# Token sums of two pairs at once, one more pair-of-pairs by seven products, and a first product fed in pieces

## The chip, the cores and the metric

The kernel runs on one core of a Trainium2 chip. The core has TensorE (PE: matrix products; PEld is its loading of the stationary operand), VectorE (DVE), ScalarE (ACT), GpSimd (POOL) and SyncE (SP), which work at the same time and wait for each other by semaphores. Transfers are issued from the queues of SP, ScalarE and POOL and carried by 16 DMA engines. The metric is the time of one execution on the device in microseconds (us).

## What is computed

One layer of a decoder for 256 tokens of width 2048, in float32:

```
h    = rmsnorm(x, g_mix);  proj = h @ w_in          # 2048 x 15872
x_r, g_r, q, k, v, gate_r, gate_a = split(proj)
y_r  = (gelu(g_r) * rg_lru(conv(x_r))) @ w_rnn_out  # 2816 wide
y_a  = stick_breaking_attention(norm(q), norm(k), v) @ w_attn_out
x    = x + (sigmoid(gate_r) * y_r + sigmoid(gate_a) * y_a) @ w_o
g, u = split(rmsnorm(x, g_ffn) @ w_ffn_gu)          # 2 x 5632 wide
x    = x + (silu(g) * u) @ w_ffn_down
x    = x + sigmoid(rmsnorm(x, g_ple) @ w_ple_gate) * (p @ w_ple_proj)
```

All weights are read once from HBM; the products of 256 tokens with them are nearly all of the arithmetic.

## The kernel before

**Products in split form.** TensorE takes float32 rounded to a shorter format (fp32r). Every operand is therefore split into a rounded part and the rest: ScalarE copies it to fp32r (`whi`, `shi`), VectorE subtracts that from the original (`wlo`, `slo`). A product is three matmuls, hi x hi, hi x lo, lo x hi, added up in PSUM (`prod`, line 207). A plain product has a tile of 128 x 128 token values as the stationary operand and 512 weight columns as the moving one. A weight tile is 128 x 1024 values, 512 KB: one load, one ScalarE copy, one VectorE subtraction.

**Groups.** `group` (line 757) computes 256 tokens times 1024 columns over all rows of a weight matrix. The rows are taken in tiles of 128, and two tiles are a pair. A pair is done plainly, by eight products (2 row tiles x 2 column halves x 2 token halves), or, where the configuration `CFG` lists it, by seven products of sums (Strassen's scheme, names `11`, `21`, `22`, `T1` to `T4`). `CFG` lists 196 pairs. The seven-product form needs sums of weight blocks and sums of token blocks.

- The weight sums `T1` to `T4` are made on VectorE (`r<-r,r`, 1024 columns), or, where the `how` list names them, by a transfer of POOL that adds a block from HBM onto the one in SBUF (`add`, line 192). Two pairs share each of these tiles.
- The token sums are made by `half_sums` (line 714) for one pair at a time: one VectorE instruction on 256 columns, two on 128, a ScalarE copy of 512 and a VectorE subtraction of 512. For the input x the unsplit tile `h` is first put together again from its two parts by VectorE (`x_sums`, line 883).

**Order of the work.** `build` writes the whole layer down as a list of operations. TensorE's come in the order of the program: the projection groups (five for the recurrent branch, a half one, two for gate_r, the recurrent output between them), then v, q and k, gate_a, the attention output, `w_o`, eleven groups for the gate and up matrices with the down products between them, and the last gate. Hooks put transposes and attention steps between the products; the positions are `att0`, `every`, `at` and `turn`. `schedule` (line 308) then plays this list through with estimated durations and with the buffers that there are (`ROOM`: 54 tiles of 1024 columns, 8 PSUM banks): each of the other engines takes what is ready in the order of due times, which are counted back from the product that needs it. TensorE may take a product up to 60 places ahead. `improve` (line 508) repeats this up to 20 times with earlier due times for whatever made TensorE wait. The result is a fixed order per engine. Waits between engines follow from the data and from buffers used again.

**The start.** Nine products on zeros (`warm`, line 648) run first. ScalarE's queue loads the 16 columns of factors `gm`. SP's queue loads the first x tile in two halves and the weights of the first two row tiles as four pieces of 512 columns. ScalarE and VectorE scale and split x (`gained`, line 705).

**The end.** The last of the four output pieces is computed in two halves of 256 columns and stored by SP (`store`, line 188), one store behind the other.

```
717:        q = tile("hs", "H")
720:        pr.vec(2 * P, lambda nc: nc.vector.tensor_tensor(
721:            R3(2)(q[:2 * P].ap()), R3(2)(h[:2 * P].ap()), R3(3)(h[P:].ap())[:, ::2, :], ALU.subtract),
723:        tt(s2, s1, a11, ALU.subtract, name="hs")
724:        tt(s4, a12, s2, ALU.add, name="hs")
725:        t = split(q.all, name)
```

Of the kernel before, what the change touches and what calls it, by code (L numbers as in the profile page):

```python
# [91 lines left out]
class Program:  # L92
# [95 lines left out]
    def store(self, dst, i, kb, name="", writes=(), cap=None):  # L188
        return self.op("SP", 0.06, 0.0, lambda nc: nc.sync.dma_start(dst(nc), i.ap()), [i], list(writes), size=kb,
                       name=name, cap=cap)  # L190
# [397 lines left out]
def order_of(ks, nd, lead=0):  # L588
# [24 lines left out]
def build(cfg):  # L613
# [11 lines left out]

    gm = const("gm", KD)
# [22 lines left out]
    pr.mms([(warm[i % 8].all, ones_r.all, nil.all, 0.4, True, True) for i in range(9)], [ones_r.all, nil.all],  # L649
# [21 lines left out]
    def load_x(i, halves=False):  # L671
        xt[i] = tile("xt", "H")
        for e in range(2) if halves else (None,):
            o = xt[i].all if e is None else xt[i][e * 256:e * 256 + 256]
            pr.load(o, dram("xT", (lambda e: lambda a: a[:, 2 * i:2 * i + 2, :].rearrange("p k s -> p (k s)")
                                   if e is None else a[:, 2 * i + e, :])(e)), 256 if e is None else 128, name="xt")

    load_x(0, True)
# [26 lines left out]
    def gained(src, gain, name):  # L705
        t = tile(name, "L", dt=F32R)
        for e in range(2):
            s = slice(e * 256, e * 256 + 256)
            g = gain[e:e + 1]
            act(t[s], src[s], AF.Identity, scale=g, name=name)  # L710
            stt(t[512 + e * 256:768 + e * 256], src[s], g, t[s].f32(), ALU.mult, ALU.subtract, name=name)
        return t

    def half_sums(h, name):


        q = tile("hs", "H")
        a11, a12 = h[:P], h[2 * P:3 * P]
        s3, s1, s2, s4 = (q[c * P:c * P + P] for c in range(4))
        pr.vec(2 * P, lambda nc: nc.vector.tensor_tensor(  # L720
            R3(2)(q[:2 * P].ap()), R3(2)(h[:2 * P].ap()), R3(3)(h[P:].ap())[:, ::2, :], ALU.subtract),
               [h.all], [q[:2 * P]], name="hs")
        tt(s2, s1, a11, ALU.subtract, name="hs")
        tt(s4, a12, s2, ALU.add, name="hs")
        t = split(q.all, name)
        return [(t[c * P:c * P + P], t[512 + c * P:640 + c * P]) for c in (1, 2, 0, 3)]
# [30 lines left out]
    def group(w, cols, ks, pairs, sums, tokens, how, hooks=None, lead=0):  # L757
# [7 lines left out]
        early = {x for x in order if x[0] in "AB"} if lead and nd else ()  # L765
# [13 lines left out]
        for n, x in enumerate(order):  # L779
# [3 lines left out]
            m, dp = x[:2]  # L783
            if m in ("A", "B"):
# [95 lines left out]
    for i in range(NPD):  # L880
        xg.append(gained(xt[i].all, gm[2 * i:2 * i + 2], "xg"))

    def x_sums(ps):
        for p in ps:
            if p not in xsum:
                h = tile("h", "H")
                tt(h.all, xg[p][:512].f32(), xg[p][512:].f32(), ALU.add, name="h")
                xsum[p] = half_sums(h, "xs")

    x_sums(xp)  # L890
    for b in range(4):
        for t in range(2):
            q = tile("xq", "H")
            pr.load(q.all, dram("x", (lambda t, b: lambda a: a[t * P:t * P + P, b * 512:b * 512 + 512])(t, b)), 256,
                    name="xq", early=None)
# [35 lines left out]
    xc, xcs, y, ysum, hr = {}, {}, [], {}, {}  # L931

# [54 lines left out]
    def finish(p):  # L987
# [4 lines left out]
        tt(r.all, ps.all, r.all, ALU.mult, name="y")  # L992
        y.append(split(r.all, "y"))
        if p in union("ro"):
            ysum[p] = half_sums(r, "ys")
# [114 lines left out]
    heads, osum = {}, {}  # L1110
    qs, ks_, zst, ost = {}, {}, {}, []
# [95 lines left out]
    def att_o(hp):  # L1207
# [18 lines left out]
        if hp in union("ao"):  # L1226
            h = tile("h", "H")
            act(h.all, ps.all, AF.Copy, name="h")
            ost.append(split(h.all, "ost"))
            osum[hp] = half_sums(h, "os")  # L1230
# [56 lines left out]
    mix, msum = {}, {}  # L1287

    def next_mix(p):
        def run():  # L1290
# [6 lines left out]
            if p in union("wo"):  # L1297
                h = tile("h", "H")
                act(h.all, ps.all, AF.Copy, name="h")
                mix[p] = split(h.all, "mix")  # L1300
                msum[p] = half_sums(h, "ms")
# [32 lines left out]
    def next_h(hs, sums, p, gcol, pairs, name):  # L1334
        def run():
            ps = turned(p, name + "t")
            g = pc(gcol, 2 * p, 2)
            if p in pairs:
                h = tile("h", "H")
# [3 lines left out]
                hs[p] = split(h.all, name)  # L1343
                sums[p] = half_sums(h, name + "s")
# [4 lines left out]
    hg, hsum = {}, {}  # L1349
    for g in range(2):  # L1350
# [11 lines left out]
        for p in range(4 * g, 4 * g + 4):  # L1362
            pend.append(next_h(hg, hsum, p, PC_GF, union("gu"), "hg"))
# [4 lines left out]
    h3, sum3 = {}, {}  # L1368
    q_of = [q for q in range(len(FQ)) for _ in range(FQ[q])]
    f0 = [sum(FQ[:q]) for q in range(len(FQ))]  # L1370
    dn_pairs = {p for v in cfg["dn"] for u in v for p in u}

    def gu(g):
# [13 lines left out]
        def turn(f):  # L1387
            def run():
# [4 lines left out]
                if p in dn_pairs:  # L1393
                    h = tile("h", "H")
                    act(h.all, ps.all, AF.Copy, name="h")
                    acts[p] = split(h.all, "act")
                    asum[p] = half_sums(h, "as")
# [6 lines left out]
    def down(q, g):  # L1404
# [19 lines left out]
        if q == len(FQ) - 1:  # L1424
            for p in range(4 * g, 4 * g + 4):
                pend.append(next_h(h3, sum3, p, PC_GP, union("pg"), "h3"))
# [142 lines left out]
```

## Time and profile before

| | |
|---|---|
| three runs | 1792.18, 1794.31, 1794.45 us; median 1794.31 |
| the profiled execution | 1792.39 us, its span 1790.7 us |
| TensorE busy | 1779.9 us, 8295 matmuls |
| VectorE busy | 1675.0 us |
| ScalarE busy | 1423.0 us |
| POOL busy | 202.6 us |
| granted TensorE clock | 0.999 |

The span runs from the first to the last instruction. TensorE's busy time is not the time that it needs at best, because matmuls overlap and their ends are modelled; how many follow each other in how much time says more. A row of the timeline gives the start, the duration, the engine, the line and operation, output<-input, the shape and the number; in square brackets stands the idle time before it and what ended it. Lines 146, 150, 179 and 215 are helpers that record all operations of a kind, so the names tell what is meant. Buffers are shared by tiles of different names: `pair` is any tile of 512 columns, and `q` and `u` are PSUM banks of the products.

### The profile page before, as it was taken

How to read it: one execution, taken by the hardware profiler on the slowest of the kernel's cores; microseconds unless marked ns; L12 is line 12 of the kernel's file. 1: busy time of each engine (PE TensorE's matmuls, PEld its weight loads, DVE VectorE, ACT ScalarE, POOL GpSimd, SP SyncE). 2: the span in 40 equal slices, each digit the busy share in tenths (PEclk: the TensorE clock that was granted, in tenths of full speed). 3: DMA queues.
4: the chain of work that ended last, by engine and by line, in shares of the span. 5: the costliest groups of instructions: out<-in, count | busy, mean ns of one | idle time of the engine just before them, and what ended most of it. 6: DMA issues, size and time to landing. Idle time of an engine off the chain costs nothing.

```text
span 1790.7 us, 23886 instructions
## 1 busy us (share of the span) xinstructions
PE 1779.9 (99%) x8295; PEld 1483.2 (83%) x8295; DVE 1675.0 (94%) x1933; ACT 1423.0 (79%) x1962; POOL 202.6 (11%) x239
## 2 busy tenths in 40 slices
PE   9999999999999999999999999999999999999998
PEld 7888888888888888888888888888888788888887
DVE  8999887998799899899999999999999898999989
ACT  8999999876567799999777878677677666778875
POOL 0000000011011100111101011101211001120110
PEclk9999999999999999999999999999999999999999
DMA  9886877769999885888979999988999878999894
GB/s 358 277 223 206 231 224 204 232 181 278 279 253 251 239 219 166 225 231 224 254 233 288 264 272 282 236 250 252 310 262 248 234 216 254 280 264 300 244 282 118
DMA packets 126842, 440.54 MB, mean 246 GB/s; under 512 B 14208, under 2 KB 14848, under 8 KB 126720
## 3 DMA queue, kind: packets, MB, share of 16 engines
q1 hardware_dynamic: 93312, 322.07, 50.4%
q0 software_dynamic: 33264, 116.93, 35.3%
q8 instruction: 65, 1.06, 0.2%
q14 instruction: 57, 0.47, 0.1%
q10 hardware_dynamic: 144, 0.01, 0.0%
HBM read 430.56 MB, written 8.39 MB: 245 GB/s over the span
## 4 chain that ended last, share of the span: by engine, by line
PE 90%; ACT 4%; DMA 2%; DVE 2%; issue 1%; SPq 0%; DVEq 0%; ACTq 0%
PE q L215 55%; PE u L215 29%; PE rg L962 2%; DMA r<-in_w_dram 1%; ACT pair L179 1%; ACT L179 1%; ACT shi L179 1%; DMA raw<-in_w_dram 1%; DVE slo L146 1%; ACT whi L179 1%; PE z L204 1%; PE o L204 1%; PE gut L224 1%; PE e L204 0%; DVE pair L146 0%
## 5 line engine op out<-in xcount | busy, mean ns | idle before, releaser
L146 DVE TENSOR_TENSOR slo<-r,shi 128x1024 fp32r<-128x1024 f32 x686 | 814.3, 1222 | 47.8 <-ACT shi L179 45.1
L179 ACT ACTIVATE shi<-r 128x1024 fp32r<-128x1024 f32 x686 | 701.5, 1055 | 181.6 <-DMA r<-in_w_dram 89.4
L146 DVE TENSOR_TENSOR wlo<-raw,whi 128x1024 fp32r<-128x1024 f32 (+3 forms) x288 | 340.2, 1197 | 19.8 <-ACT whi L179 19.6
L193 POOL DMA_DIRECT2D r<-in_w_dram x215 | 186.6, 870 | 1447.7 <-DVE slo L146 687.7
L179 ACT ACTIVATE whi<-raw 128x1024 fp32r<-128x1024 f32 (+3 forms) x288 | 294.5, 1036 | 20.1 <-DMA raw<-in_w_dram 10.6
L215 PE MATMUL q<-whi,xg 128*128 128x512 f32 x760 | 258.8, 393 | 0.2
L146 DVE TENSOR_TENSOR r<-r,r 128x1024 f32<-128x1024 f32 x177 | 213.7, 1222 | 3.8 <-DMA r<-in_w_dram 3.6
L215 PEld LDWEIGHTS q<-whi,xg 128*128 128x128 f32 x760 | 142.7, 188 | 30.7 <-issue 0.8
L215 PE MATMUL q<-wlo,xg 128*128 128x512 f32 x380 | 148.6, 391 | 0.8 <-DVE wlo L146 0.8
L179 ACT ACTIVATE pair<-u 128x512 f32<-128x512 f32 x85 | 50.6, 595 | 50.8 <-PE u L215 50.0
L215 PE MATMUL q<-whi,hg 128*128 128x512 f32 x264 | 90.6, 391 | 0.0
L215 PE MATMUL q<-shi,hgs 128*128 128x512 f32 x264 | 88.6, 394 | 0.7 <-ACT q L179 0.7
L215 PE MATMUL q<-shi,hg 128*128 128x512 f32 x264 | 88.8, 391 | 0.0
L215 PE MATMUL q<-shi,xs 128*128 128x512 f32 x256 | 88.7, 396 | 0.0
L215 PE MATMUL q<-shi,xg 128*128 128x512 f32 x252 | 86.2, 393 | 0.0
L215 PE MATMUL u<-shi,hgs 128*128 128x512 f32 x264 | 85.9, 390 | 0.0
L215 PE MATMUL u<-shi,xs 128*128 128x512 f32 x256 | 84.7, 391 | 0.0
L215 PEld LDWEIGHTS q<-wlo,xg 128*128 128x128 f32 x380 | 71.5, 188 | 15.7 <-DVE wlo L146 1.9
L215 PE MATMUL u<-whi,xg 128*128 128x512 f32 x200 | 76.0, 391 | 0.0
L215 PE MATMUL q<-whi,act 128*128 128x512 f32 x216 | 73.3, 390 | 0.0
L179 ACT ACT_TABLE_LOAD x52 | 66.7, 1283 | 2.5 <-PEq L1556 1.2
L146 DVE TENSOR_TENSOR pair<-pair,pair 128x128 f32<-128x128 f32 (+1 forms) x156 | 60.6, 413 | 8.4 <-ACT pair L179 7.9
(331 smaller groups left out, 3709.1 us busy)
## 6 DMA issues: line engine op xcount, KB each, us to landing
r<-in_w_dram SPq DMA_DIRECT2D x308, 512.0 KB, 7.4
raw<-in_w_dram SPq DMA_DIRECT2D x262, 512.0 KB, 6.1
r<-in_w_dram POOLq DMA_DIRECT2D x215, 512.0 KB, 8.7
raw<-in_w_dram SPq DMA_DIRECT2D x16, 448.0 KB, 5.0
pair<-in_x_dram SPq DMA_DIRECT2D x16, 256.0 KB, 7.5
kept<-pair POOLq DMA_DIRECT2D x16, 256.0 KB, 8.2
kept<-pair SPq DMA_DIRECT2D x8, 256.0 KB, 5.5
pair<-kept SPq DMA_DIRECT2D x8, 256.0 KB, 6.3
```

Source lines behind the costliest of these rows:

```text
L146: return self.vec(n, lambda nc: nc.vector.tensor_tensor(o.ap(), a.ap(), b.ap(), op), [a, b], [o], name=name, **kw)
L179: nc.scalar.activation(o.ap(), i.ap(), f, **kw)
L193: return self.op("POOL", 0.85, 0.0, lambda nc: nc.gpsimd.dma_start(o.ap(), src(nc), accum_op=ALU.add), list(reads), [o], size=-kb, name=na ...
L204: nc.tensor.matmul(o.ap(), l.ap(), r.ap(), start=start, stop=stop, skip_group_check=True)
L215: nc.tensor.matmul(ps.ap(), x[i].ap(), w[j].ap(), start=a, stop=b, skip_group_check=True)
L224: nc.tensor.transpose(ps[n * P:n * P + P].ap(), s.ap(), ident.ap())
L962: nc.tensor.matmul(ps.ap(), wt[i].ap(), x[j].ap(), start=a and n == 0, stop=b and n == 2, skip_group_check=True) for n, (i, j) in enumerat ...
```

## The change

It has seven parts.

1. **Token sums of two pairs at once.** `half_sums` takes a whole tile with the h of two neighbouring pairs. It makes one VectorE instruction of 512 columns in place of two of 256, two of 256 in place of four of 128, and one copy and one subtraction of 1024 in place of two of 512 each. The class `Halves` gives both pairs one tile and starts the sums when the second is there.
2. **The h of x.** For the pairs that `xr` and `gtr` list, ScalarE makes h straight from the loaded x by two scaled copies of 256 columns; VectorE no longer adds the two parts.
3. **198 pairs.** The fourth group of `xr` has six pairs in place of four.
4. **Which sums POOL makes.** The `how` lists change: gtr 0 loses T1, T2 and T3; v 0 loses T1; qk 1 gains T2; qk 2 loses T1; ro 0 gains T4; wo 0 loses T1; gu 7 has T2 in place of T4.
5. **The first transfers.** The first x tile and its column of factors come as one transfer of 129 KB on ScalarE's queue, ahead of `gm`. The weights of the first row tile come in pieces of 256, 256 and 512 columns, those of the second in one of 1024; the products of both are written in these pieces (`AB`). There are six warming products.
6. **The last store.** The second half of the last output piece is stored from ScalarE's queue.
7. **Positions.** `att0` is 3, and `turn` is [3, 4, 5, 6]. Up to seven loads of x for the norm are cut in two, so that the number of loads and stores is a multiple of 8. The planner runs over the new list, so every engine's order may differ.

The diff, cut to its core:

```diff
-    def store(self, dst, i, kb, name="", writes=(), cap=None):
-        return self.op("SP", 0.06, 0.0, lambda nc: nc.sync.dma_start(dst(nc), i.ap()), [i], list(writes), size=kb,
+    def store(self, dst, i, kb, name="", writes=(), cap=None, eng="SP"):
+        e = {"SP": "sync", "ACT": "scalar"}[eng]
+        return self.op(eng, 0.06, 0.0, lambda nc: getattr(nc, e).dma_start(dst(nc), i.ap()), [i], list(writes),
...
-        p[:2] = [(h, k) for k in p[0][1:] for h in "AB"]
+        p[:2] = [("AB", k) for k in p[0][1:]]
...
+    x0 = tile("x0", "H")
+    pr.load(x0[:S + 1], dram("x0", lambda a: a), 129, "ACT", name="x0")
...
-    pr.mms([(warm[i % 8].all, ones_r.all, nil.all, 0.4, True, True) for i in range(9)], [ones_r.all, nil.all],
+    pr.mms([(warm[i % 8].all, ones_r.all, nil.all, 0.4, True, True) for i in range(6)], [ones_r.all, nil.all],
...
+    class Halves:
...
+        def slot(self, p):
+            if not self.both(p):
+                return tile("h", "H").all
+            if p // 2 not in self.tiles:
+                self.tiles[p // 2] = tile("h", "L")
+            return self.tiles[p // 2][p % 2 * 512:p % 2 * 512 + 512]
+
+        def done(self, p, h):
+            self.seen.add(p)
+            if not self.both(p):
+                half_sums(h, 1, [p], self.sums, self.name)
+            elif p ^ 1 in self.seen:
+                half_sums(self.tiles.pop(p // 2).all, 2, [p & ~1, p | 1], self.sums, self.name)
+
+    def half_sums(h, n, ps, sums, name):
+        q = tile("hs", "L" if n == 2 else "H").all
+        cut = lambda x: x.rearrange("p (g c q) -> p g c q", g=n, c=4)
+        pr.vec(2 * P * n, lambda nc: nc.vector.tensor_tensor(
+            cut(q.ap())[:, :, 0:2], cut(h.ap())[:, :, 0:2], cut(h.ap())[:, :, 1::2], ALU.subtract), [h], [q], name="hs")
+        pr.vec(P * n, lambda nc: nc.vector.tensor_tensor(
+            cut(q.ap())[:, :, 2], cut(q.ap())[:, :, 1], cut(h.ap())[:, :, 0], ALU.subtract), [h, q], [q], name="hs")
+        pr.vec(P * n, lambda nc: nc.vector.tensor_tensor(
+            cut(q.ap())[:, :, 3], cut(h.ap())[:, :, 2], cut(q.ap())[:, :, 2], ALU.add), [h, q], [q], name="hs")
...
+            hi, lo = tile(name, "L", dt=F32R).all, tile(name, "L", dt=F32R).all
+            act(hi, q, AF.Copy, name=name)
+            tt(lo, q, hi.f32(), ALU.subtract, name=name)
...
+            if m == "AB":
+                cut = [(0, 256), (256, 512), (512, 1024)] if x is order[0] else [(0, 1024)]
+                all_ = [(w, x[1], c) for b in cols for c in b]
+                r, hi, lo = tile("raw", "L"), tile("whi", "L", dt=F32R), tile("wlo", "L", dt=F32R)
+                for a, z in cut:
+                    pr.load(r[a:z], pr.chunk(all_[a // P:z // P])[0], (z - a) // 2, name="raw")
+                for a, z in [y for a, z in cut for y in ([(a, z)] if z - a <= 512 else [(a, 512), (512, z)])]:
+                    s = slice(a, z)
+                    act(hi[s], r[s], AF.Copy, name="whi")
+                    tt(lo[s], r[s], hi[s].f32(), ALU.subtract, name="wlo")
+                    for t, ps in enumerate(((q2, q4 if x in early else U), (q3, q8))[a // 512]):
+                        pr.prod(ps[a % 512:a % 512 + z - a], tok(tokens, x[1], t), (hi[s], lo[s]), name="plain")
+                continue
...
+            if raw and p:
+                for e in range(2):
+                    s = slice(e * 256, e * 256 + 256)
+                    act(h[s], xt[p][s], AF.Identity, scale=gm[2 * p + e:2 * p + e + 1], name="h")
+            else:
+                tt(h, xg[p][:512].f32(), xg[p][512:].f32(), ALU.add, name="h")
+            hs.done(p, h)
...
-                    t, 1024 * g + 512 * b, s)), d[s], (s.stop - s.start) // 2, name="out")
+                    t, 1024 * g + 512 * b, s)), d[s], (s.stop - s.start) // 2, name="out",
+                         eng="ACT" if s.start else "SP")
...
-CFG = dict(xr=[X2, X2, X4, X4, X4], ro=[F6, F4], gtr=[X4] * 2, v=[X6, X8], qk=[X4, X6, X4, X4], gta=[X4] * 2,
+CFG = dict(xr=[X2, X2, X4, X6, X4], ro=[F6, F4], gtr=[X4] * 2, v=[X6, X8], qk=[X4, X6, X4, X4], gta=[X4] * 2,
...
-           [[16, 17, 18, 19]] * 2], how=dict(xr=[NONE, LATER, SOON, TWO, SOON], gtr=[SOON, ONE], v=[TWO] * 2,
-           qk=[SOON, TWO, TWO, ONE], gta=[ALL, LATER], ro=[TWO, ALL], ao=[TWO, SOON], wo=[TWO] * 2, gu=[TWO,
-           SOON, TWO, LATER, TWO, TWO, TWO, LATER, TWO, TWO, LATER], pg=[ALL, TWO], dn=[ONE, NONE, TWO]),
-           lead=8, order=('g1', 'r0', 'r1'), att0=4, every=9, at=(0, 4, 10, 16), turn=[3, 5, 7, 9])
+           [[16, 17, 18, 19]] * 2], how=dict(xr=[NONE, LATER, SOON, TWO, SOON], gtr=[NONE, ONE], v=[ONE, TWO],
+           qk=[SOON, SOON, ONE, ONE], gta=[ALL, LATER], ro=[LATER, ALL], ao=[TWO, SOON], wo=[ONE, TWO], gu=[TWO,
+           SOON, TWO, LATER, TWO, TWO, TWO, SOON, TWO, TWO, LATER], pg=[ALL, TWO], dn=[ONE, NONE, TWO]), lead=8,
+           order=('g1', 'r0', 'r1'), att0=3, every=9, at=(0, 4, 10, 16), turn=[3, 4, 5, 6])
```

More of the change, by code (lines that the diff above doesn't have):

```diff
@@ L708, in gained @@
             s = slice(e * 256, e * 256 + 256)
-            g = gain[e:e + 1]
-            act(t[s], src[s], AF.Identity, scale=g, name=name)
-            stt(t[512 + e * 256:768 + e * 256], src[s], g, t[s].f32(), ALU.mult, ALU.subtract, name=name)
-        return t
[L714 to L726, printed above, removed]
+            v, g = first if first and not e else (src[s], gain[e:e + 1])
@@ L1226, in att_o @@
         if hp in union("ao"):
[L1227 to L1230, printed above, removed]
+            h = oh.slot(hp)
+            act(h, ps.all, AF.Copy, name="h")
+            ost.append(split(h, "ost"))
+            oh.done(hp, h)
         else:
@@ L1297, in run @@
             if p in union("wo"):
[L1298 to L1301, printed above, removed]
+                h = mh.slot(p)
+                act(h, ps.all, AF.Copy, name="h")
+                mix[p] = split(h, "mix")
+                mh.done(p, h)
             else:
@@ L1342, in run @@
                     act(h[s], ps[s], AF.Identity, scale=g[e:e + 1], name="h")
-                hs[p] = split(h.all, name)
-                sums[p] = half_sums(h, name + "s")
+                hs[p] = split(h, name)
+                both.done(p, h)
             else:
```

86 lines of the change are left out of this document (54 added, 32 removed).

## The prediction

> **What bounds the kernel now.** I read the page's busy times first, then what TensorE waited for, then the stages one by one, and last the first ten and the last ten microseconds.
>
> The page:
>
> ```profile
> span 1790.7 us, 23886 instructions
> PE 1779.9 (99%) x8295; PEld 1483.2 (83%) x8295; DVE 1675.0 (94%) x1933; ACT 1423.0 (79%) x1962; POOL 202.6 (11%) x239
> ```
>
> TensorE's waits (total, times, longest), and one run of products from the chain:
>
> ```profile
> PE warm L204 <- DVE onesr L643: 1.6, 1, 1.6
> PE q L215 <- DVE wlo L146: 0.8, 1, 0.8
> PE gut L224 <- DVE pair L150: 0.7, 2, 0.4
> PE q L215 <- ACT q L179: 0.7, 1, 0.7
> PE u L215 <- ACT pair L179: 0.2, 1, 0.2
> 523.91 5.44 PE u L215 x24
> ```
>
> TensorE is the bound: 99% busy, and after the start its waits make 0.8 + 0.7 + 0.7 + 0.2 = 2.4 us. A 512-column product takes 5.44/24 = 0.227 us. So three things can move the time: the number of products, the two ends, and those 2.4 us, which could also grow. Whether they grow is up to VectorE (DVE) and ScalarE (ACT), which prepare every weight. By stage (span, then busy PE, PEld, DVE, ACT, POOL; granted clock, DMA share, GB/s):
>
> ```profile
> 22.60:48.00 25.40, 24.62 (x107) 19.61 (x106) 24.89 (x29) 23.16 (x39) 1.01 (x1) 1.00 1.04 378
> 250.00:300.00 50.00, 50.00 (x291) 44.05 (x290) 39.62 (x56) 45.44 (x64) 5.21 (x6) 1.00 0.70 194
> 300.00:350.00 50.00, 49.92 (x240) 41.47 (x239) 45.73 (x51) 48.10 (x63) 0.89 (x2) 1.00 0.71 229
> 350.00:400.00 50.00, 50.00 (x223) 41.42 (x222) 50.00 (x67) 37.09 (x49) 5.18 (x6) 1.00 0.71 192
> 1200.00:1400.00 200.00, 199.33 (x891) 164.66 (x890) 195.52 (x186) 146.28 (x166) 33.13 (x38) 1.00 0.96 268
> ```
>
> At 22.6 to 48 us DVE is busy 24.89 of 25.40 us and TensorE loses 0.78: the one place where DVE sets the pace.
>
> The profiled execution took 1792.39 us, 1.69 more than its span. The median shown is 1794.31, 1.92 above that; the runs lie at 1792.18, 1794.31 and 1794.45, so in two groups some 2 us apart.
>
> **The change part by part.**
>
> *Two pairs more by seven products.* Group 3 of the first projection goes from four pairs to six: 198 instead of 196. A pair takes seven products where plain takes eight, each three matmuls of 512 columns. So 2 x 3 x 0.227 = **-1.36 us**, all on TensorE's path. Behind it: seven weight tiles more split, four plain ones fewer.
>
> *First products in pieces.* Six 512-column matmuls become twelve of 256. Two of these follow each other in the tail fence below at 1782.44 and 1782.56, so 0.12 each: 12 x 0.12 - 6 x 0.227 = **+0.08**.
>
> *The start.*
>
> ```profile
> 0.81 0.40 ACTq L186 DMA_DIRECT2D gm<-in_prm_dram  x1
> 0.81 0.38 SPq L186 DMA_DIRECT2D raw<-in_w_dram  x1
> 3.74 0.63 ACT L179 ACTIVATE whi<-raw 128x512 fp32r<-128x512 f32 x1 [1.22 <-DMA raw<-in_w_dram]
> 3.83 1.48 PE L204 MATMUL warm<-pair,onesr 128*128 128x512 f32 x3
> 4.28 0.49 ACT L179 ACTIVATE xg<-pair,gm 128x256 fp32r<-128x256 f32 x1
> 5.11 0.63 PE L204 MATMUL warm<-pair,onesr 128*128 128x512 f32 x1
> 5.88 0.47 PE L215 MATMUL q<-whi,xg 128*128 128x512 f32 x1
> 6.19 0.40 PE L215 MATMUL q<-wlo,xg 128*128 128x512 f32 x1
> 7.63 0.50 PE L215 MATMUL q<-wlo,xg 128*128 128x512 f32 x1
> 9.30 0.30 PEld L215 LDWEIGHTS q<-whi,xg 128*128 128x128 f32 x2 [0.21 <-DVE xg L150]
> pair<-in_xT_dram SPq DMA_DIRECT2D x2, 128.0 KB, 3.8
> gm<-in_prm_dram ACTq DMA_DIRECT2D x1, 8.0 KB, 3.1
> ```
>
> The ninth warming product starts at 5.11, ends at 5.74, and the first real one follows at 5.88, though its inputs were there at 4.77 (4.28 + 0.49): warming is what holds it. The sixth starts at 3.83 and ends at 3.83 + 0.63 = 4.46; with the same 0.14 behind it TensorE is free at 4.60. The x tile with its factor, sent at 0.81 on ScalarE's queue, lands between 3.1 us (the 8 KB row) and 3.8 us (the 128 KB row) later, at 3.9 to 4.6, and is scaled 0.49 later. The first product comes at 4.6 to 5.1. Warming still paced at (5.11 - 3.83)/3 = 0.43 per product, and by 6.19 the real ones go at half that, so products up to about 6 run at half speed. From 4.7: six slow ones of 256 columns (0.21) end at 5.98, six at 0.12 at 6.7, six of 512 at 8.06. Before, the same work ended near 8.9 (5.88 + 12 x 0.227 + 0.3 of waits, the one at 7.63 among them), and the next tile waited 0.21 at 9.30. That gives 0.8 + 0.2: **-1.0**. Bounds: -1.3 with no wait, and +0.3 if the second tile, now one transfer of 512 KB where two of 256 KB were, comes last of all. I take -1.0, since its rows are those of this very start. ScalarE issues the x tile ahead of the factors and its table load (0.4 us later for both); it idles until 3.74, which covers that, and without that cover the first split would be 0.4 later.
>
> The Trainium skill ("TensorE: Matmul & The Clock Gate", "Part 1: The HAM clock gate") says that the slow phase is some 3.4 us of activity in a window that runs free of the kernel, not a count of products. The trace agrees so far: slow at 5.11, fast by 6.19. By that rule fewer warming products don't lengthen the phase, but it may end later in another execution.
>
> *The end.*
>
> ```profile
> 1782.44 0.28 PE L215 MATMUL pp<-whi,pts 128*128 128x256 f32 x1
> 1782.56 0.28 PE L215 MATMUL pp<-wlo,pts 128*128 128x256 f32 x1
> 1785.96 0.41 DVE L146 TENSOR_TENSOR pair<-pair,pair 128x256 f32<-128x256 f32 x1
> 1786.17 0.38 SPq L189 DMA_DIRECT2D out_dram<-pair  x1
> 1786.64 0.40 SPq L189 DMA_DIRECT2D out_dram<-pair  x1
> out_dram<-pair SPq DMA_DIRECT2D x2, 128.0 KB, 2.9
> ```
>
> The last half is ready at 1786.37 but its store issues at 1786.64, behind the first half's on SP. From ScalarE's queue, empty by then, it goes at about 1786.45: **-0.2**, between 0 and -0.27 if that queue lands alike; the 3.1 against 2.9 us of the two rows would eat it, so +0.2 is the upper bound.
>
> *VectorE, ScalarE, POOL.* Costs that count only where they make TensorE wait:
>
> ```profile
> L146 DVE TENSOR_TENSOR slo<-r,shi 128x1024 fp32r<-128x1024 f32 x686 | 814.3, 1222 | 47.8 <-ACT shi L179 45.1 <-PE u L215 1.3
> L146 DVE TENSOR_TENSOR r<-r,r 128x1024 f32<-128x1024 f32 x177 | 213.7, 1222 | 3.8 <-DMA r<-in_w_dram 3.6
> L720 DVE TENSOR_TENSOR pair<-pair 128x256 f32<-128x256 f32 x54 | 21.8, 422 | 0.0
> L146 DVE TENSOR_TENSOR hgs<-pair,hgs 128x512 fp32r<-128x512 f32 x8 | 5.5, 688 | 0.8 <-ACT hgs L179 0.8
> L146 DVE TENSOR_TENSOR pair<-pair,pair 128x128 f32<-128x128 f32 x106 | 27.6, 288 | 0.1
> L179 ACT ACTIVATE xg<-pair,gm 128x256 fp32r<-128x256 f32 x16 | 7.2, 495 | 0.0
> L193 POOL DMA_DIRECT2D r<-in_w_dram x215 | 186.6, 870 | 1447.7 <-DVE slo L146 687.7 <-ACT pair L179 143.0 <-ACT shi L179 95.2
> ```
>
> Two pairs' sums cost DVE 2 x (0.42 + 2 x 0.26 + 0.69) = 3.26 now, and 0.69 + 2 x 0.42 + 1.22 = 2.75 merged: 27 merges save 14 us. The merged forms aren't in the trace: the first, of 512 columns, is priced by the 512-column row (0.69) and bounded by two of the 256-column row (0.84), which would leave 10 us. Six x pairs make their h on ScalarE: DVE -6 x 0.69 = -4, ScalarE +12 x 0.495 = +6. The new lists of weight sums move work from POOL to DVE (counted from the lists: 215 adding transfers become 210, 177 sums on DVE become 186): +9 x 1.22 = +11. Three more splits: +4. The pair waits for its second half: what stands behind it on DVE is only the sum's own three steps, since other ready work is placed between. DVE ends about 3 us below its 1675. In the start stage it falls by 2 x 0.69 + 0.5 = 1.9, and needs to be 1.0 earlier, so 0.9 covers the wait of 0.8; I count **-0.6** of the 2.4, between -2.4 (all gone) and +3.0 (below). ScalarE's 23.16 of 25.40 leaves 2.2 us there for the 2.0 us of the first two pairs' h. That cover is thin.
>
> *At nothing:* up to seven more x loads on SP, which idles for free buffers; att0 and turn, which put transposes at other places between products; both hidden while TensorE has other products ready.
>
> Sum: -1.36 + 0.08 - 1.0 - 0.2 - 0.6 = **-3.1 us**. Against the profiled execution that is 1789.3, against the median 1791.2; as the runs fall in two groups I take the middle of the two, **1790.2**.
>
> **The rivals.**
>
> *R1, all waits go.* DVE is relieved in every stage that has sums, so the 2.4 us vanish whole: 1.8 more, 1788.4. For it: each of the four waits is short and on an engine that is relieved or off its limit. Against: DVE is busy 195.52 of 200 us at 1200 to 1400, where the change takes little from it, so a split that is late there stays late.
>
> *R2, gtr group 0 stalls.* It runs near 290 to 338 us, and its six sums leave POOL for DVE: +7.3 us into a stage at 45.73 of 50, 53.0 where 50 are, so 3.0 us of waiting; 1793.2. For it: 350 to 400 is full already (50.00). Against: 250 to 300 has 10 us of slack, and sums can be done ahead.
>
> *R3, the start gives nothing.* Each microsecond of slow clock past 6 us costs 0.47 (1 - 0.227/0.43), so full speed at 8.1 instead of 6 takes the whole 1.0: 1791.2. The skill's free-running window, cited above, is the rule that would do this; the trace shows one execution and can't exclude it.
>
> *R4, buffers; slower.*
>
> ```profile
> SPq L186 <- PE q L215: 560.7, 188, 18.5
> ACT shi L179 <- DMA r<-in_w_dram: 89.4, 69, 6.2
> ```
>
> SP's loads wait for buffers that products free, and the weight split waits 89.4 us for loads. A merged sum holds the first pair's h until the second's is there, and whole tiles instead of halves. If each of the 27 merges delays a load into TensorE by 0.32 us, that is 8.6: 1790.2 + 8.6 = 1798.8. From 0.29 each it is slower by 0.2%. Against: TensorE waits 2.4 us in all today, although loads came up to 6.2 us late: the stock of split weights absorbs them.
>
> **How the numbers follow.** 0.2% (3.6 us) is about what a measurement of this kernel can tell from no change: faster ends at 1790.7, slower begins at 1797.9. Forecast 0.48, with the boundary inside its own range of 1789.0 to 1791.4, so 0.30 faster and 0.18 same; R1 0.20, faster; R2 0.12 and R3 0.08, same; R4 0.12, slower. Faster 0.50, same 0.38, slower 0.12. The range runs from below R1, 1786.8, to above R2, 1794.2, and leaves R4 out.
>
> **What would show it.** A count of 8295 - 3 (warming) - 6 (pairs) + 6 (the cut) = 8292 matmuls. A first real product at 4.6 to 5.1; the last two stores issued by two queues within 0.3 us; 210 adds on POOL; 27 merged sums of 512 columns; no DVE wait near 41 us. Wrong if TensorE's waits after 10 us exceed 4 us in all, above all at 290 to 350 (R2), or as many short ones behind weight splits late by their loads (R4).

## The result and the profile after

| | before | after |
|---|---|---|
| median of seven runs | 1793.27 us (1792.18 to 1794.45) | 1787.48 us (1787.00 to 1788.65) |
| profiled execution, its span | 1792.39, 1790.7 | 1788.65, 1786.9 |

The ratio is 0.997, with a 95% interval of 0.9959 to 0.9981: 5.8 us faster where 3.1 were forecast. The profiled execution of the changed kernel is the slowest of its seven, so its span is only 3.8 us shorter. A second trace of the same kernel (first experiment) has a span of 1786.3.

The page after: busy times, and two of the costliest groups.

```profile
span 1786.9 us, 23795 instructions
PE 1777.3 (99%) x8292; PEld 1481.6 (83%) x8292; DVE 1678.2 (94%) x1832; ACT 1429.2 (80%) x1953; POOL 198.8 (11%) x234
L194 POOL DMA_DIRECT2D r<-in_w_dram x210 | 182.7, 871 | 1443.0 <-DVE slo L146 620.4
L146 DVE TENSOR_TENSOR r<-r,r 128x1024 f32<-128x1024 f32 x186 | 224.6, 1216 | 0.5 <-DMA r<-in_w_dram 0.4
```

The merged sums, from the groups by form:

```profile
L743 DVE TENSOR_TENSOR hs<-h 128x512 f32<-128x512 f32 x27 | 18.4, 682 | 1.0 <-PE u L216 0.7 <-ACT h L179 0.4
L747 DVE TENSOR_TENSOR hs<-h,hs 128x256 f32<-128x256 f32 x27 | 11.3, 418 | 0.1
L745 DVE TENSOR_TENSOR hs<-hs,h 128x256 f32<-128x256 f32 x27 | 11.3, 417 | 0.1
```

The change is there as counted: 8292 matmuls, 210 adding transfers, 186 weight sums on VectorE, 27 merges at 0.68 us. But VectorE has gained 3.2 us of work (1675.0 to 1678.2), where it was to lose 3. What TensorE waited for, and the start:

```profile
PE u L216 <- ACT pair L179: 2.8, 4, 1.1
PE warm L205 <- DVE onesr L646: 1.6, 1, 1.6
PE q L216 <- ACT u L179: 1.0, 1, 1.0
```

```profile
3.72 0.51 ACT L179 ACTIVATE xg<-pair 128x256 fp32r<-128x256 f32 x1 [0.71 <-DMA pair<-in_x_dram]
4.59 0.58 PE L216 MATMUL q<-whi,xg 128*128 128x256 f32 x1
6.80 0.42 PE L216 MATMUL q<-wlo,xg 128*128 128x512 f32 x1
7.05 0.52 PE L216 MATMUL q<-whi,xg 128*128 128x512 f32 x2
```

The first product starts at 4.59 instead of 5.88. From 6.80 to 7.05 a 512-column product takes 0.25: the full pace is there at 6.80, where before it was there at 6.19 (0.24 per product from then on). Yet TensorE's waits after the start grew, from 2.4 us to 2.8 + 1.0 = 3.8. Now the end. The chain of waits of the kernel before, from 1762.20 on (start, time, what):

```profile
1762.20 5.45 PE u L215 x24
1767.66 0.02 issue
1767.68 1.21 DVE slo L146
1768.90 1.13 DVE wlo L146
...
1779.64 0.91 DVE slo L146
...
1783.76 1.94 DVE pair L146 x4
```

and of the kernel after:

```profile
1767.83 5.44 PE u L216 x24
1773.27 2.72 PE pp L216 x12
1775.99 5.44 PE u L216 x24
1781.43 0.73 PE pp L216 x6
...
1783.50 0.42 DVE pair L146
```

This is the largest difference between the traces, and the prediction had not looked for it. Before, the chain is VectorE's from 1767.68 to its last output step, which ends at 1786.37; when TensorE is through, VectorE still has output steps of 512 columns in hand. After, the chain is TensorE's until 1782.15, and only steps of 256 columns follow. The last products of both, before and then after:

```profile
1783.76 0.28 PE L215 MATMUL pp<-whi,pts 128*128 128x256 f32 x1
```

```profile
1782.58 0.28 PE L216 MATMUL pp<-whi,pts 128*128 128x256 f32 x1
```

From the end of the last product to the end of the span it is 1790.7 - 1784.04 = 6.7 us before and 1786.9 - 1782.86 = 4.0 after. So the 3.8 us between the spans are 2.6 behind the last product and 1.2 ahead of it. Of the 2.6, VectorE's last step accounts for 1.3 (2.33 us behind the last product before, 1.06 after) and the issue of the last store behind that step for 0.2 (0.27 and 0.09). The other 1.2 lie between that issue and the end of the span (4.06 and 2.89): the last stores land after 2.9 us before and after 2.0 and 2.5 now. Before, five stores go out from 1783.87 on; after, four go out from 1780.93 on and the last at 1784.01. That fewer stores on the way make the last one faster is likely, but no run separates it.

The 1.2 ahead of the last product are not explained piece by piece. The products (-1.36 + 0.08) and the waits (+1.4) cancel, and the earlier first product has been used up a few microseconds later, as the run with the old ends will show.

The waits need their place. Busy time from 40 to 56 us (span, then busy PE, PEld, DVE, ACT, POOL; granted clock, DMA share, GB/s) before, and then after:

```profile
40.00:56.00 16.00, 15.22 (x67) 12.28 (x67) 16.00 (x20) 15.94 (x28) 0.00 (x0) 1.00 1.04 373
```

```profile
40.00:56.00 16.00, 12.94 (x55) 9.72 (x54) 14.39 (x19) 13.93 (x24) 0.00 (x0) 1.00 0.97 342
```

TensorE idles 3.06 us there after, 0.78 before, and the other engines are no longer full. The timeline after shows what it waits for, and who waited ahead of that:

```profile
41.27 1.06 ACT L179 ACTIVATE whi<-raw 128x1024 fp32r<-128x1024 f32 x1 [1.70 <-DMA raw<-in_w_dram]
44.75 0.50 PE L216 MATMUL u<-shi,xs 128*128 128x512 f32 x1 [0.99 <-ACT pair L179]
48.84 0.50 PE L216 MATMUL u<-shi,xg 128*128 128x512 f32 x1 [1.06 <-ACT pair L179]
54.92 0.50 PE L216 MATMUL q<-shi,xg 128*128 128x512 f32 x1 [1.02 <-ACT u L179]
```

A weight load is late at 41.27 and ScalarE loses 1.70; its copies out of PSUM, for which the next products wait, then come late three times.

### The profile page after: what moved, and what is told of

Read it like the earlier page. It is cut to its first block, busy times and chain, and to the rows that moved or that the text cites. A ratio compares the mean times of both kernels' runs of the same rounds, so it can differ in the third digit from the quotient of the medians.

```text
span 1786.9 us, 23795 instructions
## 1 busy us (share of the span) xinstructions
PE 1777.3 (99%) x8292; PEld 1481.6 (83%) x8292; DVE 1678.2 (94%) x1832; ACT 1429.2 (80%) x1953; POOL 198.8 (11%) x234
## 3 DMA queue, kind: packets, MB, share of 16 engines
q8 instruction: 65, 1.06, 0.2%
## 4 chain that ended last, share of the span: by engine, by line
PE 97%; DMA 1%; DVE 1%; ACT 0%; issue 0%; SPq 0%; DVEq 0%; ACTq 0%
PE q L216 59%; PE u L216 31%; PE rg L1016 3%; DMA raw<-in_w_dram 1%; PE z L205 1%; PE o L205 1%; PE pp L216 1%; PE gut L225 1%; PE e L205 0%; DVE slo L146 0%; DMA r<-in_w_dram 0%; PE hdt L225 0%; PE grt L225 0%; PE xrt L225 0%; ACT shi L179 0%
## 5 line engine op out<-in xcount | busy, mean ns | idle before, releaser
L146 DVE TENSOR_TENSOR wlo<-raw,whi 128x1024 fp32r<-128x1024 f32 (+2 forms) x285 | 334.9, 1189 | 22.9 <-ACT whi L179 22.1
L194 POOL DMA_DIRECT2D r<-in_w_dram x210 | 182.7, 871 | 1443.0 <-DVE slo L146 620.4
L179 ACT ACTIVATE whi<-raw 128x1024 fp32r<-128x1024 f32 (+2 forms) x285 | 290.4, 1035 | 34.9 <-DMA raw<-in_w_dram 22.8
L216 PE MATMUL q<-whi,xg 128*128 128x512 f32 (+1 forms) x740 | 249.7, 392 | 0.1
L146 DVE TENSOR_TENSOR r<-r,r 128x1024 f32<-128x1024 f32 x186 | 224.6, 1216 | 0.5 <-DMA r<-in_w_dram 0.4
L216 PE MATMUL q<-wlo,xg 128*128 128x512 f32 (+1 forms) x370 | 144.2, 390 | 0.0
L216 PE MATMUL u<-whi,xg 128*128 128x512 f32 x192 | 71.9, 390 | 0.0
L146 DVE TENSOR_TENSOR pair<-q,pair 128x512 f32<-128x512 f32 x89 | 59.0, 682 | 9.7 <-PE q L216 7.5
```

What stands on the lines that cost most here:

```text
L146: return self.vec(n, lambda nc: nc.vector.tensor_tensor(o.ap(), a.ap(), b.ap(), op), [a, b], [o], name=name, **kw)
L179: nc.scalar.activation(o.ap(), i.ap(), f, **kw)
L194: return self.op("POOL", 0.85, 0.0, lambda nc: nc.gpsimd.dma_start(o.ap(), src(nc), accum_op=ALU.add), list(reads), [o], size=-kb, name=na ...
L216: nc.tensor.matmul(ps.ap(), x[i].ap(), w[j].ap(), start=a, stop=b, skip_group_check=True)
```

## The experiments

Theories: (L) the x loads cut in two, and the new start, cost the time at 40 to 56 us, and without that the kernel would be faster still; (S) the gain at the end comes from VectorE's relief by the merged sums; against it (C), that it comes from the lists, the last store, the positions of hooks or the order that the planner makes. Kernels were timed in three jobs, each against the kernel before; "order kept" means that the planner's order of every engine stays that of the changed kernel, "planned anew" that it may differ.

| run | job's before | median (range; runs) | ratio to before, 95% |
|---|---|---|---|
| e1_again | 1792.87 | 1788.23 (1786.52 to 1789.16; 6) | 0.9973 (0.9962 to 0.9984) |
| e2_whole | 1792.87 | 1787.76 (1785.54 to 1788.04; 5) | 0.9968 (0.9956 to 0.9981) |
| e3_apart | 1792.87 | 1790.41 (1789.15 to 1791.62; 11) | 0.9984 (0.9975 to 0.9993) |
| e4_ends | 1792.87 | 1787.90 (1786.79 to 1788.75; 6) | 0.9970 (0.9959 to 0.9981) |
| f1_lists | 1793.31 | 1792.09 (1791.37 to 1795.34; 11) | 0.9995 (0.9986 to 1.0004) |
| f2_sums | 1793.31 | 1792.43 (1790.06 to 1793.92; 11) | 0.9994 (0.9985 to 1.0003) |
| f3_turn | 1793.31 | 1787.54 (1786.39 to 1789.14; 6) | 0.9969 (0.9957 to 0.9980) |
| f4_196 | 1793.31 | 1790.02 (1788.31 to 1792.91; 11) | 0.9982 (0.9973 to 0.9991) |
| h1_listsums | 1793.18 | 1787.98 (1787.58 to 1789.14; 6) | 0.9972 (0.9960 to 0.9983) |
| h2_hdve | 1793.18 | 1787.98 (1785.48 to 1788.46; 6) | 0.9968 (0.9955 to 0.9980) |
| h4_start | 1793.18 | 1787.18 (1786.63 to 1787.79; 5) | 0.9965 (0.9953 to 0.9978) |
| g1_nocut | 1793.18 | 1787.69 (1786.58 to 1788.76; 5) | 0.9968 (0.9955 to 0.9980) |

**The changed kernel again.** No edit; it shows how far two traces of one kernel differ.

> The changed kernel once more, for a second trace and a narrower interval. If the three waits of about 1 us each at 43 to 55 us (TensorE for ScalarE's copies out of PSUM) are a property of the order, they stand in this trace too, 2.5 to 4 us in all; if they belong to that one execution, TensorE's waits after 10 us are below 1.5 us here. Ratio to the kernel before 0.9965 to 0.998.

1788.23. TensorE's waits make 3.1 us here too, but only one of the three stands in its place (1.07 at 48.15): at 40 to 56 us it is busy 14.76 of the 16 us, not 12.94. So what is lost there differs by 1.8 us between executions of one kernel, and half a microsecond between single traces proves nothing.

**x loads whole.** Order kept; each pair of half loads becomes one.

```diff
-pr.load(q[e * 256:e * 256 + 512 // n], ...)
+o = pr.load(q[e * 256:e * 256 + 512 // n], ...)
+if n == 2:
+    o.emit = <one transfer of all 512 columns> if e == 0 else <nothing>
```

> Order of all engines kept, but the seven x loads that were cut in two are sent whole again (the first half's place sends 256 KB, the second's nothing). Theory L (late loads): with halves, as many transfers are in flight but each carries half, the rate falls to 237 GB/s at 35 to 40 us, a weight load comes 1.7 us late, ScalarE is held in order and its PSUM copies with it. Then TensorE's waits at 40 to 55 us fall from 3.3 to below 1 and the time by 1.5 to 2.5 us against the changed kernel. Rival A: ScalarE is late because it now makes h for six pairs; then the waits stay at 2.5 to 3.5 us and the time within 0.5 us.

The hole in its place does close. The window of this kernel:

```profile
40.00:56.00 16.00, 16.00 (x72) 13.17 (x71) 15.57 (x20) 15.61 (x27) 0.00 (x0) 1.00 1.03 404
```

404 GB/s instead of 342, and TensorE full. But the time, 1787.76, lies within the spread of the unchanged order, where theory L asked for 1.5 to 2.5 us less. This trace also loses time at another place, ahead of the window. Here is the 17th product in this order, in the trace of the change, in that of the old ends (below) and in this one with its successors:

```profile
8.23 0.39 PE L216 MATMUL q<-wlo,xg 128*128 128x512 f32 x1
```

```profile
8.18 0.40 PE L216 MATMUL q<-wlo,xg 128*128 128x512 f32 x1
```

```profile
9.39 0.63 PE L216 MATMUL q<-wlo,xg 128*128 128x512 f32 x1
9.82 1.05 PE L216 MATMUL q<-whi,xg 128*128 128x512 f32 x2
```

With whole loads the products keep the slow pace, 0.43 us (9.39 to 9.82) per 512 columns, until 11.09; this trace is then 1.7 us behind that of the change. That is how it comes to be only 0.19 ahead of the first experiment at the first product on `y` (378.74 against 378.93) and 1.7 ahead of the trace of the change (380.45). L is right on the place. What the place is worth stays open: the median is 0.5 us below the first experiment's, within the spread.

**Merged sums issued apart.** Order kept; each merged step is issued as two instructions of half the width, with the same values.

```diff
-tensor_tensor(cut(q)[:, :, 0:2], cut(h)[:, :, 0:2], cut(h)[:, :, 1::2], subtract)
+[tensor_tensor(one(q, g)[:, 0:2], one(h, g)[:, 0:2], one(h, g)[:, 1::2], subtract) for g in range(n)]
 ... the other two sums, the copy and the subtraction alike
```

> Order kept, but the sums of two pairs are made by two instructions each again (54 splits of 512 columns on VectorE and ScalarE, 108 and 54 small steps), so VectorE has some 14 us more, 2 of them in the last gate's stage. Theory D: the last 40 us are bound by VectorE (10.00 of 10 us busy in each slice from 1740 on, before and after), so its relief is what shortened the end; then the last output is 1.5 to 3 us later after TensorE's last product, the time 3 to 7 us longer than the changed kernel's. Rival O: the end is shorter because the planner put the last steps in another order; then the end stays within 0.5 us and the time within 1.5 us.

1790.41, 2.2 us above the first experiment in the same job, with ranges that hardly touch. This is the wider instruction alone: the waiting for the second pair is the same. It lies between the two expectations, D's 3 to 7 and O's under 1.5. Its busy times:

```profile
PE 1778.1 (99%) x8292; PEld 1480.3 (83%) x8292; DVE 1684.3 (94%) x1940; ACT 1431.2 (80%) x1980; POOL 198.3 (11%) x234
```

VectorE has 108 instructions more and is busy 6.1 us more, 0.056 each. The end of its chain is VectorE's again:

```profile
1762.32 4.09 PE u L216 x18
1766.44 1.23 DVE slo L146
```

But the stretch behind the last product grows only from 4.0 and 4.1 to 4.6 us, near O's 0.5 and not by D's 1.5 to 3. More of the loss lies ahead: TensorE waits 1.22 us at 420.32 and 0.32 at 445.42 for ScalarE's copies out of PSUM, against 0.24 and nothing in the trace of the change; the rest has no single place.

**Old ends.** Order kept; nine warming products, last store from SP.

```diff
-for i in range(6)
+for i in range(9)
-                         eng="ACT" if s.start else "SP")
+                         (issued by nc.sync)
```

> Order kept, but nine warming products and the last store from SP. The two places are apart in the trace. Start: the first real product comes at 5.8 to 5.95 in place of 4.59. If the first 55 us are bound by loads and ScalarE (theory L), most of the 1.3 us is swallowed there and the time grows by 0 to 0.5 us; the prediction's reading, a start that counts whole, gives +0.7 to +1.3. End: the last store issues 0 to 0.3 us later than at 1784.01 relative to its data (ready at 1783.92), since SP is free by then in the changed kernel: +0 to +0.3 against the prediction's +0.2.

1787.90, no slower. Its first product starts at 5.76, 1.2 us later, but the 17th at 8.18 against 8.23 (rows above). The lead of six warming products is gone by then: in the trace of the change the first seven products take 2.21 us (4.59 to 6.80), here 1.02 (5.76 to 6.78). There they go at 0.43 us per 512 columns until 6.80, and the first three start 0.5 us further apart than even that pace asks; here they go at 0.24. The first product on `y` starts at 378.60, earlier than in both traces of the change. The end:

```profile
1781.64 0.43 DVE L146 TENSOR_TENSOR pair<-pair 128x256 f32<-128x256 f32 x1
1782.09 0.33 SPq L1532 DMA_DIRECT2D out_dram<-pair  x1
```

SP issues the last store 0.02 us after its data are ready (1781.64 + 0.43 = 1782.07). The queue, then, is worth nothing here: the first half's store is long out, because VectorE no longer brings both halves within some 0.3 us.

**Lists alone, sums alone, both.** The kernel before with the new `CFG` only (198 pairs, `how`, `att0`, `turn`); the kernel before with the merged sums only; with both, but the old start, h of x on VectorE, whole x loads and SP's store. Planned anew.

```diff
-CFG = dict(xr=[X2, X2, X4, X4, X4], ...)
+CFG = dict(xr=[X2, X2, X4, X6, X4], ...)
```

```diff
-def half_sums(h, name):
+class Halves: ...
+def half_sums(h, n, ps, sums, name):
```

> The kernel before with the new lists alone (198 pairs, which sums POOL makes, att0, turn), planned anew; sums still pair by pair, old start, old store. Theory D (VectorE's relief by merged sums is what the lists need): the lists give VectorE nine sums and three splits more, 15 us, and no relief, so the two products saved (-1.4 us) are lost again: 1792 to 1795 us, and the stretch from TensorE's last product to the end stays above 5.5 us (6.66 before). Rival T (the new turn puts the h of the last gate's second half 8 us earlier and VectorE ahead): 1788.5 to 1791, that stretch below 5 us.

> The kernel before with merged token sums alone, planned anew; old lists, old start, old store. Theory D: VectorE has 14 us less, TensorE's waits after 10 us shrink below 1.5 us and the end by 1 to 2 us: 1789 to 1791. Rival T: the end stays at 6 us or more and the time at 1791 to 1793.

> The kernel before with the new lists and the merged sums together; old start, h of x by VectorE, x loads whole, last store from SP. Alone the lists gave -1.2 us and the sums -0.9 (1793.3 before). Theory S, the parts only add: 1790.7 to 1792. Theory I, the lists' products come through only with VectorE relieved, and the short end (4.0 to 4.5 us after the last product) with them: 1788.5 to 1790.2.

Alone they give 1.2 and 0.9 us, neither outside its interval; together 5.2, which is all of the gain and below both ranges of the last expectation. (Its theory S, that the parts only add, is not the S of this section.) The sums alone came out mixed: the time is rival T's, the short end theory D's. Single traces say where, if cut at the start of the last product on `act` (the last down product; 1691.84 before, 1690.73 after):

| trace | up to there, against before | from there to the end of the span | of it behind the last product |
|---|---|---|---|
| before | 0 | 98.9 | 6.7 |
| lists alone | -2.2 | 100.7 | 7.2 |
| sums alone | +0.8 | 97.7 | 4.5 |
| both | -2.8 | 96.7 | 4.5 |
| after | -1.1 | 96.2 | 4.0 |
| after, again | -1.8 | 96.2 | 4.1 |
| sums issued apart | +0.1 | 96.7 | 4.6 |
| 196 pairs | +0.3 | 96.6 | 4.4 |

The first column differs by 0.7 us between the two traces of the change, the other two by 0.1 at most. In these traces the lists win ahead of the last stage and lose it inside; the merged sums win inside. Together both wins stay. VectorE is what they share. From 1740 to 1784 us it is busy 44.00 us before, with the lists alone and with the sums alone; with both:

```profile
1740.00:1784.00 44.00, 41.16 (x188) 34.14 (x186) 42.02 (x45) 25.14 (x29) 3.48 (x4) 1.00 0.50 120
```

That is no idle time: with both, VectorE's last step ends at 1782.23, so 42.02 is all but full as well. Its busy share doesn't tell these kernels apart; the chain does. With the lists alone it is VectorE's from 1750.45 on, with both TensorE's to the last product:

```profile
1750.45 0.63 DVE r L146
```

```profile
1779.73 0.73 PE pp L216 x6
```

Without merged sums the end is long (6.7 and 7.2), with them it is short in every run (4.0 to 4.6), whatever the lists, the store or the positions. So the end comes with the merged sums. The wider instruction is a part of that: undoing it with the order kept puts VectorE back on the chain, but gives back only 0.5 us of the last stage. The other 2 us or so go with the order that the planner makes of the merged sums, or with stores that don't crowd; no run separates these. S is shown in part. Why the sums alone lose 0.8 us ahead of the last stage is open: TensorE's listed waits are 0.4 us more than before and the first product 0.05 earlier, which leaves 1.4 us of its end, 1.8 us later, unexplained. Each of these kernels is planned anew, so its order differs too.

**Positions.** The change with the old `turn`, planned anew.

```diff
-turn=[3, 4, 5, 6]
+turn=[3, 5, 7, 9]
```

> The changed kernel with the old turn ([3, 5, 7, 9]), planned anew. Rival T: the stretch from the last product to the end grows from 4.0 to 5.5 to 6.7 us and the time by 1.5 to 2.5 us. Theory D: stretch and time stay within 0.8 us of the changed kernel.

1787.54, and 4.5 us behind the last product: nothing that rival T expected.

**196 pairs.** The change without its two new pairs, planned anew.

```diff
-xr=[X2, X2, X4, X6, X4]
+xr=[X2, X2, X4, X4, X4]
```

> The changed kernel with four pairs in xr's fourth group (196), planned anew. Two products more on TensorE: +1.36 us where nothing else moves; TensorE's six matmuls more (8298). The prediction's term holds if the time is 0.7 to 2.0 us above the changed kernel; if VectorE or ScalarE bound that stage (their work falls by 4 and 3 us), it is within 0.5 us.

1790.02, so the two pairs are worth 2.5 us, more than the 0.7 to 2.0 expected, and 1.36 of it by their products; the table puts the loss ahead of the last stage (+0.3 against -1.1 and -1.8). The other 1.1 us may be the new order; nothing in its waits (2.3 us) shows it.

**h of x by VectorE; the old start; no cut loads.** Three times the change with one part undone, planned anew.

```diff
 h of x:      -if raw and p:              +if False:
 old start:   -p[:2] = [("AB", k) ...]    +p[:2] = [(h, k) ... for h in "AB"]
              -pr.load(x0...)             +x tile in two halves; nine warming products
 no cuts:     -"cuts": -n % 8             +"cuts": 0
```

> The changed kernel with the h of x put together by VectorE again, planned anew: VectorE 4 us more, ScalarE 6 less. If the move to ScalarE earns its place: +1 to +2.5 us, with TensorE waiting for VectorE's weight splits in the first 100 us. If it doesn't (ScalarE's own lateness at 43 to 55 us costs as much): within 0.7 us of the changed kernel's 1787.7, and the waits for ScalarE's PSUM copies there fall below 1.5 us.

> The changed kernel with the old start: x tile in two halves by SP, factors apart, four weight pieces of 512, nine warming products, 24 products ahead of the first seven-product block in place of 32; planned anew. First real product at 5.4 to 5.9. The prediction's reading (-1.0 us for the start): 1788.4 to 1789.2. From the run with nine warming products, where 1.2 us at the start were gone by 380 us: within 0.5 us of 1787.7.

> The changed kernel with all eight x loads whole, planned anew. Theory L: TensorE's waits at 40 to 56 us are below 0.7 us (1.2 to 3.1 in the changed kernel) and the time 0.5 to 1.5 us shorter, 1786.2 to 1787.2, which would beat both kernels. If the cut serves the end (number of loads and stores a multiple of 8), the stretch after the last product grows by 0.5 us or more and the gain is lost.

1787.98, 1787.18, 1787.69: none differs from the change by more than its spread. Without the cut loads TensorE is busy 15.74 of 16 us at 40 to 56 and the profiled execution is at 1786.58, but the median isn't lower, and above theory L's 1786.2 to 1787.2; the stretch behind the last product is 4.5 us, as with the whole loads in the kept order. With the h of x on VectorE and the loads still cut, TensorE is busy 15.80 of the 16 us. So either of the two, undone, closes the hole there in its trace, and neither shortens the time by what the runs can tell.

## Why the prediction was right and where it was wrong

The side was right, and the time, 2.7 us below the forecast, is inside its range. The terms did worse than the sum, and that they made a time inside the range is luck in part.

*Two pairs, -1.36.* Right in sign, too small: undoing them costs 2.5 us, and only the products were in the sum.

*First products in pieces and the start, +0.08 and -1.0.* The step to the first product held: 4.59, the lower edge of 4.6 to 5.1. The step that failed is the next one, "From 4.7: six slow ones of 256 columns (0.21) end at 5.98 [...] six of 512 at 8.06". The slow pace lasted until 6.80 and the first three products came 0.5 us late behind each other, so the eighteen products were through at 8.70, against 8.89 before: 0.2 us, not 0.8. The other 0.2, the wait at 9.30, didn't go either (9.58 - 8.93 for two products that take 0.46 at full pace). The old start gives 1787.18 and nine warming products 1787.90, so the start is worth nothing measurable. That is R3's outcome, and the slow pace that R3 named is a part of the cause; in two other traces with six warming products it lasted longer still (last section).

*The end, -0.2.* The step that failed is the first one of all, "TensorE is the bound", read from 99% busy and 2.4 us of waits. No wait of TensorE can show that VectorE is behind once no product needs it any more. The chain of before shows it, from 1767.68 on. The term had the store's queue in it, which is worth 0.1 at most, and neither VectorE's backlog nor the last store's way, which made 1.3 and 1.2 of the 2.6 us in these traces. The last two stores came 0.8 us apart (1783.19 and 1784.01), not within 0.3: the halves now come as TensorE delivers them.

*VectorE's sum.* "27 merges save 14 us" added up row durations. The rows overlap: in the timeline after, a split that starts at 1776.69 and takes 1.22 is followed by the next instruction at 1777.83, so it holds the engine 1.14.

```profile
1776.69 1.22 DVE L146 TENSOR_TENSOR slo<-r,shi 128x1024 fp32r<-128x1024 f32 x1
1777.83 0.68 DVE L146 TENSOR_TENSOR pair<-q,pair 128x512 f32<-128x512 f32 x1
```

Measured, merging saves 6.1 us (apart against after) to 6.5 (sums alone against before: 1675.0 to 1668.5). The lists add 11.1 (1686.1 with them alone), where +11 for sums and +4 for splits were forecast, and h of x takes 2.4 off VectorE (1680.6 to 1678.2), not 4. -6.5 + 11.1 - 2.4 makes +2.2; the page has +3.2. The Trainium skill ("Vector Engine (DVE) Microarchitecture Reference", "5.2 Measured stream behaviour on trn2 (trn3 not measured)") gives some 75 ns per instruction after the overlap of the queue, measured there on 32-bit integers, so 108 x 0.075 = 8.1 us as an estimate. That is nearer than the 14, and the runs have 6.1.

*TensorE's waits, -0.6.* They grew, by 1.4 us in the first trace and 0.7 in the second (3.1). The wait for VectorE near 41 us did go. ScalarE, whose cover I called thin, took its place. Late loads have a share in it (16.00 and 15.74 of 16 us busy with whole loads), and so, by the one trace there is, has the h of x (15.80 with that back on VectorE, planned anew); which of them starts it is open, and the time is the same without either.

*At nothing: x loads, positions.* For the time that holds, for the loads and for `turn`. In the trace the cut loads do show, and they were costed without a look at how SP's loads wait for each other (last section).

*R1* didn't come, though its 1788.4 is the nearest number. *R2*: the work came, the stall didn't. After:

```profile
250.00:300.00 50.00, 50.00 (x290) 43.95 (x289) 44.38 (x61) 47.06 (x66) 0.00 (x0) 1.00 0.59 187
300.00:350.00 50.00, 50.00 (x243) 41.72 (x242) 49.70 (x57) 48.96 (x63) 0.86 (x1) 1.00 0.61 205
```

VectorE's 8.7 us more (44.38 - 39.62 and 49.70 - 45.73) are spread over both windows, and TensorE is full in both: the slack named against R2 was used. *R4*: no sign; the waits stay under the 4 us that would have spoken for it, and their last cause is ScalarE in 40 to 56 us, not splits held up by merges.

The sum came out on the right side because a term that wasn't there (-2.6 at the end) outweighed two that were (-1.0 at the start, -0.6 for the waits). With the products these terms as measured make -1.36 + 0.08 - 2.6 + 1.4 = -2.5 us; the profiled executions differ by 3.8, so 1.3 has no place yet. The two pairs at 2.5 would nearly fill it, but the run that gives the 2.5 is planned anew.

## What to carry to other kernels

TensorE, 99% busy, didn't set the end of this kernel, because VectorE, which drains it, was behind at the last instruction: read the last 30 us of the chain before any term is summed. A busy share that is full in every variant tells nothing; compare the chains. An earlier first product counts only if the products behind it find their operands and the full pace; follow the same product through two traces of one order to see when the lead is gone. Two changes that each stayed within their intervals gave the whole gain together, so undo them in pairs as well as singly.

## What was not expected of the hardware

*SP had at most eight transfers under way.* From issue to landing it is never more in any of the fourteen traces. The x loads around the late weight load, in halves:

```profile
34.75 3.83 SPq L186 DMA_DIRECT2D pair<-in_x_dram  x7
```

```profile
SPq L186 <- DMA raw<-in_w_dram: 2.7, 1, 2.7
```

Seven halves go out in 3.83 us, behind a weight load of 33.44 that follows six other halves. The eighth half waits 2.7 us, until that load has landed (at 41.24); it is the load for which ScalarE waits until 41.27. With whole loads in the same order it goes out at 29.79. So each half takes one of eight places and carries half as much. From 35 to 40 us the core moves 237 GB/s, and 300 with whole loads in the same order:

```profile
35.00:40.00 5.00, 5.00 (x24) 4.14 (x23) 4.70 (x7) 4.50 (x10) 0.00 (x0) 1.00 0.92 237
```

```profile
35.00:40.00 5.00, 5.00 (x24) 4.14 (x23) 4.70 (x7) 4.94 (x11) 0.00 (x0) 1.00 1.06 300
```

The second trace of the change has 280 there. Whether the eight are the chip's or the program's, no run here tells.

*Which queue stores last.* The Trainium skill ("DMA: Bandwidth & Descriptors", "Issuing engines are not separate DMA queues") says that issuing from several engines saves only the sequencer's time to start a transfer. The old-ends run agrees: from SP the last store goes 0.02 us after its data, from ScalarE 0.09 after them (1783.50 + 0.42 = 1783.92, then 1784.01), and the stretch behind the last product is 4.1 and 4.0 us.

*Executions of one kernel differ in two places.* One is the stage at 40 to 56 us, where loads come just in time: 1.8 us between two traces of the changed kernel, of the size of the spread of its runs (1786.52 to 1789.16). The other is the start. With six warming products the full pace comes between 5.4 and 6.8 us in six traces, at 9.84 in that of the h of x by VectorE and at 11.09 in that of the whole loads, the last with the order of the change; with nine it is there by 6.9 in all six traces. The granted clock reads 1.00 from 4 to 12 us all the same. So few traces can't say how often the long phase comes.
